# A two-layer decoder trunk: the turned copy of h in front of the gated input embedding is made through memory instead of on TensorE

## The chip, the cores and the metric

The kernel runs on one core of a Trainium2 chip. The metric is the device time of one execution in microseconds (us): the median of three runs before the change is 986.39 us (985.43 to 986.48). The profile shows one further execution, taken by the hardware profiler. Engines are named as the profile names them: PE is TensorE (PEld its weight loads), DVE is VectorE, ACT is ScalarE, POOL is GpSimd, and SP is the queue that issues nearly all transfers.

## The reference

The reference computes two layers over 256 tokens of width 1024 in float32. A layer has a gated feed-forward block (FFN 1), a token mixer, a second feed-forward block (FFN 2) and a gated per-layer input embedding. The change lies where the last two meet:

```python
h = h + 0.5 * swiglu(rms_norm(h, ffn2_norm), ffn2_w_gate, ffn2_w_up, ffn2_w_down)

gate = jax.nn.sigmoid(rms_norm(h, ple_norm) @ w_ple_gate)
h = h + gate * (p_i @ w_ple_proj)
```

`w_ple_gate` is 1024 x 1024 and `w_ple_proj` 256 x 1024. After the second layer a last RMS norm gives the output.

## The kernel before, in words

**Numbers.** Each float32 operand of a matmul is split into a high part and a remainder (tile names end in h and l), and each product is three matmuls: high times high, high times low, low times high (`mm3`, lines 263 to 268). So each piece of weights needs two instructions after it has landed: ACT copies the high part (`wh`, line 161) and DVE subtracts it to get the low part (`wl`, line 162). A piece is 128 x 1024 numbers, 512 KB, loaded by one transfer on SP (line 157) into one of seven raw buffers; the parts go into one of eight pairs of part buffers. The raw buffer comes free when `wl` is done, the part buffers when the last matmul has read them.

**Tiles.** The 256 tokens are two tiles t = 0 and 1 of 128. h is kept with tokens on partitions, in two halves f of 512 columns each. As the stationary operand of a matmul it must stand the other way round, with its columns on partitions: x, in parts h and l, eight chunks k of 128 columns. `turn_h` (line 379) makes one tile and half of x: four PE transposes (line 385) into one PSUM bank, four ACT copies that scale by the norm's gain (line 390, tile `xf`), an ACT copy to the high part (line 392) and a DVE subtraction for the low part (line 393).

**The end of FFN 2.** Its last product runs in `lagging` (line 423): four chunks of weights for tile 0, and the same four for tile 1, three chunks later. Each chunk and tile is six matmuls into two PSUM banks. When a tile's last chunk is done, `residual` (line 412) adds the two banks to h on DVE (line 416), and puts `turn_h` for both halves on a list of things to be emitted a little later, counted in matmul time (`soon`, `tick`); the turns of tile 0 fall between tile 1's last matmuls, those of tile 1 among the first matmuls of the next stage. ACT also sums the squares of h for the norm (`junk`, line 354), whose factor is applied later, as the scale of the sigmoid.

**The gates.** `ple` (line 1083) loops over halves f of the output columns and, within, over tiles t. Each half first computes the projection of the extra input p, `pv`, twelve matmuls for both tiles, and then for each tile the gate `e`: 8 chunks k x 3 = 24 matmuls over all of x. So the first half's gate weights (two units of two pieces) serve both tiles before the second half's are needed. Behind each `e` come the sigmoid on ACT (`se`, line 1113), the product with `pv` on DVE (`me`, line 1115) and the sum into h (line 1116). In the first layer each new part of h is then turned on PE for the next layer (`xt_e`); in the second, the last one, it is scaled and leaves.

**What sets the order.** The program is written as one sequence; a scheduler puts each engine's instructions into a fixed order, shown below where it changes, and every engine follows its own in order. The gates inside the FFNs already go through memory in the way that the change now uses for h (lines 549 to 558): DVE turns 32 x 32 blocks (`STREAM_TRANSPOSE`), one transfer writes the tile to memory (`m`), and four transfers of 64 KB read it back rearranged (`ft`).

## Time and profile before

| what | value |
|---|---|
| median of three runs | 986.39 us |
| profiled execution, its own time | 986.46 us |
| its span | 984.7 us |
| PE busy | 974.3 us (99%) |
| DVE busy | 844.6 us (86%) |
| ACT busy | 640.9 us (65%) |
| transfers | 208.32 MB, mean 212 GB/s |
| granted TensorE clock | 0.998 of full speed |

The busy time of PE says little, since matmuls overlap: one of 512 columns lasts 0.39 us in the records, but the next starts 0.227 us after it. A lost time on PE shows as a larger distance between two starts, and the prediction reads these distances. The first layer's stretch from the end of FFN 2 to the end of the gates lies at 451 to 493 us, the second layer's at 936 to 977 us. In names of tiles in the profile the layer is left out of some: d_b and xt_b belong to FFN 2, pv and e to the gates, g_a to the next FFN 1.

### The profile page before, as it was taken

How to read it: one execution, taken by the hardware profiler on the slowest of the kernel's cores; microseconds unless marked ns; L12 is line 12 of the kernel's file. 1: busy time of each engine (PE TensorE's matmuls, PEld its weight loads, DVE VectorE, ACT ScalarE, POOL GpSimd, SP SyncE). 2: the span in 40 equal slices, each digit the busy share in tenths (PEclk: the TensorE clock that was granted, in tenths of full speed). 3: DMA queues.
4: the chain of work that ended last, by engine and by line, in shares of the span. 5: the costliest groups of instructions: out<-in, count | busy, mean ns of one | idle time of the engine just before them, and what ended most of it. 6: DMA issues, size and time to landing. Idle time of an engine off the chain costs nothing.

```text
span 984.7 us, 13887 instructions
## 1 busy us (share of the span) xinstructions
PE 974.3 (99%) x4872; PEld 821.3 (83%) x4872; DVE 844.6 (86%) x1035; ACT 640.9 (65%) x958; POOL 39.1 (4%) x55
## 2 busy tenths in 40 slices
PE   9999999999999999999999999999999999999996
PEld 8888888899888888887878888889998888888885
DVE  5799899966789998989889989998666999987994
ACT  6756566857596556557866655667757865755673
POOL 0000000100110000000110000001010100000010
PEclk9999999999999999999999999999999999999999
DMA  8948766763065878576748786668602667876551
GB/s 300 357 159 295 243 198 216 262 227 109 23 234 157 268 254 276 156 246 215 256 144 278 227 277 212 210 213 299 210 27 86 214 205 243 278 239 207 200 199 43
DMA packets 85173, 208.32 MB, mean 212 GB/s; under 512 B 13680, under 2 KB 33264, under 8 KB 85104
## 3 DMA queue, kind: packets, MB, share of 16 engines
q1 hardware_dynamic: 84672, 206.87, 63.2%
q8 instruction: 38, 0.62, 0.3%
q10 hardware_dynamic: 432, 0.57, 0.2%
q14 instruction: 31, 0.25, 0.1%
HBM read 195.87 MB, written 11.53 MB: 211 GB/s over the span
## 4 chain that ended last, share of the span: by engine, by line
PE 80%; DVE 9%; DMA 4%; ACT 3%; issue 3%; SPq 0%; POOL 0%; POOLq 0%; DVEq 0%; ACTq 0%
DMA raw<-in_w 3%; PE g_a L267 3%; PE g_a L265 3%; PE g_a L266 3%; PE p_a L267 3%; PE p_a L266 3%; PE p_a L265 3%; PE d_a L267 3%; PE d_a L265 3%; PE d_a L266 3%; PE u_a L266 3%; PE u_a L265 3%; PE u_a L267 3%; PE p_b L265 3%; PE p_b L267 2%
## 5 line engine op out<-in xcount | busy, mean ns | idle before, releaser
L162 DVE TENSOR_TENSOR wl<-raw,wh 128x1024 fp32r<-128x1024 f32 (+1 forms) x278 | 320.7, 1186 | 56.1 <-ACT wh L161 55.0
L161 ACT ACTIVATE wh<-raw 128x1024 fp32r<-128x1024 f32 (+1 forms) x278 | 279.0, 1035 | 83.1 <-DMA raw<-in_w 19.4
L202 ACT ACTIVATE wh<-raw 128x1024 fp32r<-128x1024 f32 x133 | 139.4, 1060 | 128.8 <-DVE raw L197 75.5
L203 DVE TENSOR_TENSOR wl<-raw,wh 128x1024 fp32r<-128x1024 f32 x133 | 159.8, 1217 | 13.4 <-ACT wh L202 12.0
L197 DVE TENSOR_TENSOR raw<-raw,raw 128x1024 f32<-128x1024 f32 x76 | 92.6, 1220 | 4.8 <-DMA raw<-in_w 4.1
L265 PE MATMUL d_a<-wh,fh_a 128*128 128x512 f32 x108 | 42.4, 392 | 0.0
L266 PE MATMUL d_b<-wl,fh_b 128*128 128x512 f32 x108 | 42.2, 391 | 0.1
L267 PE MATMUL d_b<-wh,fl_b 128*128 128x512 f32 x108 | 42.3, 391 | 0.0
L265 PE MATMUL d_b<-wh,fh_b 128*128 128x512 f32 x108 | 42.2, 391 | 0.0
L267 PE MATMUL d_a<-wh,fl_a 128*128 128x512 f32 x108 | 42.1, 389 | 0.0
L266 PE MATMUL d_a<-wl,fh_a 128*128 128x512 f32 x108 | 42.0, 389 | 0.0
L265 PE MATMUL g_a<-wh,x0h 128*128 128x512 f32 x80 | 31.2, 393 | 0.0
L267 PE MATMUL g_a<-wh,x0l 128*128 128x512 f32 x80 | 31.0, 390 | 0.0
L266 PE MATMUL g_a<-wl,x0h 128*128 128x512 f32 x80 | 31.0, 389 | 0.0
L266 PE MATMUL u_a<-wl,x0h 128*128 128x512 f32 x64 | 25.0, 391 | 0.0
L265 PE MATMUL u_a<-wh,x0h 128*128 128x512 f32 x64 | 25.0, 394 | 0.0
L265 PE MATMUL g_b<-wh,x_mix1h 128*128 128x512 f32 x64 | 25.0, 391 | 0.0
L265 PE MATMUL g_b<-wh,x_mix0h 128*128 128x512 f32 x64 | 25.0, 391 | 0.0
L266 PE MATMUL g_b<-wl,x_mix1h 128*128 128x512 f32 x64 | 25.0, 391 | 0.0
L265 PE MATMUL g_a<-wh,xe0h 128*128 128x512 f32 x64 | 25.0, 391 | 0.0
L266 PE MATMUL g_b<-wl,x_mix0h 128*128 128x512 f32 x64 | 25.0, 390 | 0.0
L267 PE MATMUL u_a<-wh,x0l 128*128 128x512 f32 x64 | 24.9, 390 | 0.0
(527 smaller groups left out, 2672.1 us busy)
## 6 DMA issues: line engine op xcount, KB each, us to landing
raw<-in_w SPq DMA_DIRECT2D x338, 512.0 KB, 5.4
m_b<-pr_b SPq DMA_DIRECT2D x20, 256.0 KB, 2.3
ft_b<-m_b SPq DMA_DIRECT2D x80, 64.0 KB, 3.2
raw<-in_w SPq DMA_DIRECT2D x16, 256.0 KB, 5.0
m_a<-pr_a SPq DMA_DIRECT2D x16, 256.0 KB, 2.5
ft_a<-m_a SPq DMA_DIRECT2D x64, 64.0 KB, 2.8
xin<-in_xT SPq DMA_DIRECT2D x4, 256.0 KB, 5.0
h<-in_xr SPq DMA_DIRECT2D x2, 512.0 KB, 8.9
```

The source lines that it names most:

```text
L161: nc.scalar.activation(wh[:, a], r[:, a], AF.Copy),
L162: nc.vector.tensor_tensor(wl[:, a], r[:, a], wh[:, a].bitcast(F32), ALU.subtract),
L197: nc.vector.tensor_tensor(self.raw[o], self.raw[a], self.raw[b], op)
L202: newest_wh[0] = nc.scalar.activation(wh, r, AF.Copy)
L203: nc.vector.tensor_tensor(wl, r, wh.bitcast(F32), ALU.subtract)
L265: nc.tensor.matmul(o, ah, bh, start=start, stop=False, **kw)
L266: nc.tensor.matmul(o, ah, bl, start=False, stop=False, **kw)
L267: newest_mm[0] = nc.tensor.matmul(o, al, bh, start=False, stop=stop, **kw)
```

## The change

`move_h` takes the place of `turn_h` behind FFN 2. For each tile and half DVE turns the blocks into a buffer `hb`, a transfer writes it to memory (`mh`, 256 KB), and, after a delay, four transfers read it back (`hf`, 64 KB each); ACT scales `hf` in place, four instructions, and copies the high part, and DVE subtracts. The columns of x stand in another order than before, so the rows of the gate weights and the gains are permuted to match, ahead of the launch. The lag in front of it goes from 3 chunks to 4, so all of tile 0's chunks stand before tile 1's. In `ple` the projection `pv` is computed for both halves and both tiles at once, 24 matmuls; then the loop runs over tiles outside and halves inside, so all four units of gate weights are needed within tile 0. The transfers of the second half's weights stand behind the reads of tile 0 (`load_fence`). The delays of the turns for the next layer change.

```diff
+        def fetch(self, q, i):
...
+            newest_load[0] = nc.sync.dma_start(r, w[self.u, :, a : a + n])
+            if load_fence[0] is not None:
+                after(newest_load[0], load_fence[0])
...
+    def move_h(x, t, n, gcol, name):
...
+        pr = flat("w1", f"hb{t}{n}_{name}")
+        turned = nc.vector.transpose(pr, h[:, t, half(n)])
+        m = mem_p.tile([P, 4, P], F32, tag="turn", name=f"mh{t}{n}_{name}")
+        nc.sync.dma_start(m, pr.rearrange("p (q r) -> p q r", q=4))
+        a = wt("w2", f"hf{t}{n}_{name}", 4, P)
+
+        def back():
+            for q in range(4):
+                i = nc.sync.dma_start(a[32 * q : 32 * q + 32], m[:, q].rearrange("(a f) r -> f a r", a=4))
+            if t == 0:
+                newest_back[0] = i
+
+        def parts():
+
+            f = a.rearrange("p a (j s) -> p j a s", j=4)
+            c = gcol + 4 * n
+            for j in range(4):
+                nc.scalar.activation(f[:, j], f[:, j], AF.Copy, scale=g_sb[:, c + j : c + j + 1])
+            xh, xl = (in_runs(q) for q in both(x, slice(None), slice(4 * n, 4 * n + 4), slice(t * P, (t + 1) * P)))
+            two = nc.scalar.activation(xh, f, AF.Copy), nc.vector.tensor_tensor(xl, f, xh.bitcast(F32), ALU.subtract)
...
+        soon(BACK + 0.1 * n, back)
+        soon(PARTS + 0.1 * n, parts)
...
-            soon(wait[f], lambda f=f: turn_h(x, t, f, gcol, tag))
+            if far:
+                done = move_h(x, t, f, gcol, tag)
+            else:
+                soon(wait[f], lambda f=f: turn_h(x, t, f, gcol, tag))
...
-        return lagging(rest, d, gates, 0.5, tag, gcol, 3, False)
+
+        return lagging(rest, d, gates, 0.5, tag, gcol, 3 if between is None else 4, False, between is not None)
...
-        for f in range(2):
-            c = half(f)
-            wf = wide([Unit(4) for _ in range(2)])
-            v = [bank(f"pv{L}{f}{t}") for t in range(2)]
-            for k in range(2):
-                for t in range(2):
-                    mm3(v[t], tok(xp, k, t), up.at(k, c.start, c.stop), k == 0, k == 1, skip_group_check=True)
+        us = [[Unit(4) for _ in range(2)] for f in range(2)]
+        wf = [wide(u) for u in us]
+        up.ready()
+        us[0][0].ready()
+        for q in range(2):
+            us[0][1].fetch(q, 0)
+
+        load_fence[0] = newest_back[0]
+        for u in us[1]:
+            for q in range(2):
+                u.fetch(q, 0)
+        v = [[bank(f"pv{L}{f}{t}") for t in range(2)] for f in range(2)]
+        for k in range(2):
             for t in range(2):
+                for f in range(2):
+                    mm3(v[f][t], tok(xp, k, t), up.at(k, f * 512, (f + 1) * 512), k == 0, k == 1, skip_group_check=True)
+        for t in range(2):
+            for f in range(2):
+                c = half(f)
...
-                        soon(4.4 if f == 0 else 2.8, lambda t=t, f=f: turn_h(nx, t, f, gcol, f"e{L}"))
+                        soon(4.4 if t else 7.0 - f, lambda t=t, f=f: turn_h(nx, t, f, gcol, f"e{L}"))
```

The change moves instructions on three engines. The places below are those of the first layer, where FFN 2 meets the gates; the second layer's read alike. In the names, d_b000 to d_b011 are the PSUM banks of tile and half, 80 is the unit of the projection's weights, 81 and 82 are those of the first half's gates, 83 and 84 of the second half's, and the digit behind the unit is the piece. First DVE. Before:

```order
L416 SCALAR_TENSOR_TENSOR h_84<-d_b000_3969,h_84 128x512
L416 SCALAR_TENSOR_TENSOR h_84<-d_b001_3970,h_84 128x512
L162 TENSOR_TENSOR wl80_0_0_198_4485<-raw80_0_0_198_4486,wh80_0_0_198_4484 128x1024
L162 TENSOR_TENSOR wl80_1_0_199_4509<-raw80_1_0_199_4510,wh80_1_0_199_4508 128x1024
L416 SCALAR_TENSOR_TENSOR h_84<-d_b010_3971,h_84 128x512
L393 TENSOR_TENSOR x_b0l_4387<-xf00_b0_4433,x_b0h_4386 128x4x128
L416 SCALAR_TENSOR_TENSOR h_84<-d_b011_3972,h_84 128x512
L162 TENSOR_TENSOR wl81_0_0_200_4534<-raw81_0_0_200_4535,wh81_0_0_200_4533 128x1024
```

On the same engine at the same place, now:

```order
L457 SCALAR_TENSOR_TENSOR h_84<-d_b000_3969,h_84 128x512
L457 SCALAR_TENSOR_TENSOR h_84<-d_b001_3970,h_84 128x512
L409 STREAM_TRANSPOSE hb00_b0_4415<-h_84 128x512
L409 STREAM_TRANSPOSE hb01_b0_4421<-h_84 128x512
L457 SCALAR_TENSOR_TENSOR h_84<-d_b010_3971,h_84 128x512
L457 SCALAR_TENSOR_TENSOR h_84<-d_b011_3972,h_84 128x512
L172 TENSOR_TENSOR wl80_0_0_333_4489<-raw80_0_0_334_4486,wh80_0_0_333_4488 128x1024
L409 STREAM_TRANSPOSE hb10_b0_4465<-h_84 128x512
L409 STREAM_TRANSPOSE hb11_b0_4471<-h_84 128x512
L172 TENSOR_TENSOR wl80_1_0_335_4495<-raw80_1_0_336_4492,wh80_1_0_335_4494 128x1024
L172 TENSOR_TENSOR wl81_0_0_337_4501<-raw81_0_0_338_4498,wh81_0_0_337_4500 128x1024
L172 TENSOR_TENSOR wl81_1_0_339_4507<-raw81_1_0_340_4504,wh81_1_0_339_4506 128x1024
```

The two low parts of unit 80 have moved from ahead of tile 1's sums to behind them, and four block transposes have come in. Next PE, from the last matmul of FFN 2 on. Before:

```order
L266 MATMUL d_b011_3972<-wl79_1_0_197_4368,fh_b0_4_3854 128x512
L267 MATMUL d_b011_3972<-wh79_1_0_197_4367,fl_b0_4_3855 128x512
L265 MATMUL pv000_4482<-wh80_0_0_198_4484,xpsbk0_4263 128x512
L266 MATMUL pv000_4482<-wl80_0_0_198_4485,xpsbk0_4263 128x512
L267 MATMUL pv000_4482<-wh80_0_0_198_4484,xpv0_4264 128x512
L265 MATMUL pv001_4483<-wh80_0_0_198_4484,xpsbk0_4263 128x512
```

On PE, now:

```order
L276 MATMUL d_b011_3972<-wl79_1_0_331_4370,fh_b0_4_3854 128x512
L277 MATMUL d_b011_3972<-wh79_1_0_331_4369,fl_b0_4_3855 128x512
L275 MATMUL pv000_4522<-wh80_0_0_333_4488,xpsbk0_4263 128x512
L275 MATMUL pv010_4524<-wh80_0_0_333_4488,xpsbk0_4263 128x512
L275 MATMUL pv001_4523<-wh80_0_0_333_4488,xpsbk0_4263 128x512
L275 MATMUL pv011_4525<-wh80_0_0_333_4488,xpsbk0_4263 128x512
L276 MATMUL pv000_4522<-wl80_0_0_333_4489,xpsbk0_4263 128x512
```

Four matmuls that need only the high part now stand before the first that reads `wl80`. Last the SP queue, which before held only weight loads here (unit 82, then 83 and on). Now:

```order
L155 DMA raw82_1_0_342_4512<-in_w 128x1024
L411 DMA mh00_b0_4417<-hb00_b0_4415 128x512
L411 DMA mh01_b0_4423<-hb01_b0_4421 128x512
L416 DMA hf00_b0_4419<-mh00_b0_4417 32x4x128 x4
L416 DMA hf01_b0_4425<-mh01_b0_4423 32x4x128 x4
L411 DMA mh10_b0_4467<-hb10_b0_4465 128x512
L411 DMA mh11_b0_4473<-hb11_b0_4471 128x512
L155 DMA raw83_0_0_343_4514<-in_w 128x1024
L155 DMA raw83_1_0_344_4516<-in_w 128x1024
L155 DMA raw84_0_0_345_4518<-in_w 128x1024
L155 DMA raw84_1_0_346_4520<-in_w 128x1024
L416 DMA hf10_b0_4469<-mh10_b0_4467 32x4x128 x4
```

The four loads of the second half's weights have moved behind the writes of all of h and the reads of tile 0, and ahead of the reads of tile 1.

More of the change, by code (lines that the diff above doesn't have):

```diff
@@ L135, in trunk @@
     newest_load, newest_wh, newest_wl = [None], [None], [None]
+    load_fence, newest_back, far_parts = [None], [None], [None, None]
     fence = [None, None]
@@ L146, in __init__ @@
             self.sub, self.cut = sub, cut
-            self.parts, self.here = {}, set()
+            self.parts, self.here, self.raw = {}, set(), {}
+        def fetch(self, q, i):
+            n = PIECE // self.sub
+            name = f"raw{self.u}_{q}_{i}_{next(ids)}"
+            r = self.raw[q, i] = raw_p.tile([P, PIECE], F32, tag="raw", name=name)[:, :n]
+            a = q * PIECE + i * n
+            newest_load[0] = nc.sync.dma_start(r, w[self.u, :, a : a + n])
+            if load_fence[0] is not None:
+                after(newest_load[0], load_fence[0])
         def load(self, q, i):
             name = f"{self.u}_{q}_{i}_{next(ids)}"
+            if (q, i) not in self.raw:
+                self.fetch(q, i)
             if q not in self.parts:
@@ L154, in load @@
             wh, wl = (t[:, i * n : (i + 1) * n] for t in self.parts[q])
-            r = raw_p.tile([P, PIECE], F32, tag="raw", name=f"raw{name}")[:, :n]
-            a = q * PIECE + i * n
-            newest_load[0] = nc.sync.dma_start(r, w[self.u, :, a : a + n])
+            r = self.raw.pop((q, i))
             for c in range(self.cut):
@@ L393, in turn_h @@
         nc.vector.tensor_tensor(xl, f, xh.bitcast(F32), ALU.subtract)
+    def move_h(x, t, n, gcol, name):
[16 more added lines that the diff above has]
+            two = nc.scalar.activation(xh, f, AF.Copy), nc.vector.tensor_tensor(xl, f, xh.bitcast(F32), ALU.subtract)
+            if t == n == 0:
+                fence[:] = two
+            far_parts[:] = two
+        soon(BACK + 0.1 * n, back)
+        soon(PARTS + 0.1 * n, parts)
+        return turned
     def column(r, name, behind):
@@ L410, in four, with residual @@
         return [[bank(f"{name}{t}{n}") for n in range(2)] for t in range(2)]
-    def residual(x, n, d, t, scale, tag, gcol, wait=(1.2, 1.9)):
+    def residual(x, n, d, t, scale, tag, gcol, far, wait=(1.2, 1.9)):
         for f in range(2):
@@ L421, in residual, with lagging @@
         return done
-    def lagging(chunks, d, x, scale, tag, gcol, lag, first=True, behind=True):
+    def lagging(chunks, d, x, scale, tag, gcol, lag, first=True, far=False, behind=True):
         nx, nn = new_x(f"x_{tag}"), Norm(tag)
@@ L432, in lagging @@
                     if c == N - 1:
-                        done = residual(nx, nn, d, t, scale, tag, gcol)
+                        done = residual(nx, nn, d, t, scale, tag, gcol, far)
                         if t == 0 and behind:
@@ L1063, in mix @@
         rest = [(us[2 + i // 2], i % 2, 4 + i) for i in range(4)]
-        return lagging(rest, d, Of(y), 1.0, f"mix{L}", g0 + G_FFN2, 4, False, False)
+        return lagging(rest, d, Of(y), 1.0, f"mix{L}", g0 + G_FFN2, 4, False, behind=False)
     def ple_inputs(L):
@@ L1108, in ple @@
                     for k in range(KC):
-                        mm3(e, tok(x, k, t), both(wf(k), slice(None), p), k == 0, k == KC - 1, skip_group_check=True)
-                    if f == t == 0:
-                        flush()
+                        mm3(e, tok(x, k, t), both(wf[f](k), slice(None), p), k == 0, k == KC - 1, skip_group_check=True)
                     s = flat("w0", f"se{L}{f}{t}{a}")[:, :step]
@@ L1114, in ple @@
                     m = flat("w1", f"me{L}{f}{t}{a}")[:, :step]
-                    nc.vector.tensor_tensor(m, v[t][:, p], s, ALU.mult)
+                    product = nc.vector.tensor_tensor(m, v[f][t][:, p], s, ALU.mult)
+                    if f and not t:
+                        after(sig, far_parts[0])
+                        after(product, far_parts[1])
                     nc.vector.tensor_tensor(hc, m, hc, ALU.add)
@@ L1120, in ple @@
                     else:
-                        soon(4.4 if f == 0 else 2.8, lambda t=t, f=f: turn_h(nx, t, f, gcol, f"e{L}"))
-                if f:
-                    nn.done(t)
-                    if last:
-                        leave(hg, nn, t)
+                        soon(4.4 if t else 7.0 - f, lambda t=t, f=f: turn_h(nx, t, f, gcol, f"e{L}"))
+            nn.done(t)
+            if last:
+                leave(hg, nn, t)
         if not last:
@@ L1233, in _weights, with _far @@
         for m in range(0, DM, 512):
-            wide(i["w_ple_gate"][L], ar(m, m + 512))
+            wide(i["w_ple_gate"][L][_far()], ar(m, m + 512))
     return np.stack(units)
+def _far():
+    import numpy as np
+    return np.concatenate([k + turned_order(512) for k in range(0, DM, 512)])
 def _gains(i):
@@ L1241, in _gains @@
     names = ("ffn1_norm", "mix_norm", "q_lat_norm", "kv_lat_norm", "sb_out_norm", "mla_out_norm", "ffn2_norm", "ple_norm")
-    g = [i[n][L].reshape(-1, P) for L in range(DEPTH) for n in names] + [i["final_norm"].reshape(-1, P)]
+    g = [i[n][L][_far() if n == "ple_norm" else slice(None)].reshape(-1, P) for L in range(DEPTH) for n in names] + [i["final_norm"].reshape(-1, P)]
     return np.ascontiguousarray(np.concatenate(g).T)
```

## The prediction

> **What bounds the kernel now.** I read the page's busy times first, then the busy time in a stretch over the place of the change, then PE's own timeline there, start by start.
>
> ```profile
> PE 974.3 (99%) x4872; PEld 821.3 (83%) x4872; DVE 844.6 (86%) x1035; ACT 640.9 (65%) x958; POOL 39.1 (4%) x55
> ...
> 460.00:480.00 20.00, 19.89 (x96) 15.75 (x95) 18.28 (x20) 17.60 (x43) 3.81 (x4) 1.00 0.71 238
> ```
>
> In the row of the stretch the columns are the stretch, its length, then busy time (and count) of PE, PEld, DVE, ACT and POOL, the granted clock, the transfers' share and GB/s. PE is busy for 19.89 of 20 us, but DVE is for 18.28 as well. So PE sets the end, and taking work from it pays, provided DVE, which gets more work, doesn't become what PE waits for. PE's timeline (start, duration, line, tile) shows what the removed transposes cost:
>
> ```profile
> 460.25 0.39 PE L266 MATMUL d_b<-wl,fh_b 128*128 128x512 f32 x1
> 460.48 0.60 PE L385 MATMUL xt_b<-c_sb,h 128*128 128x128 f32 x4
> 460.83 0.48 PE L267 MATMUL d_b<-wh,fl_b 128*128 128x512 f32 x1
> 461.15 0.60 PE L385 MATMUL xt_b<-c_sb,h 128*128 128x128 f32 x4
> 461.50 0.48 PE L265 MATMUL d_b<-wh,fh_b 128*128 128x512 f32 x1
> 461.82 0.39 PE L266 MATMUL d_b<-wl,fh_b 128*128 128x512 f32 x1
> ...
> 462.75 0.39 PE L267 MATMUL d_b<-wh,fl_b 128*128 128x512 f32 x1
> 462.98 0.39 PE L265 MATMUL pv<-wh,xpsbk 128*128 128x512 f32 x1
> ```
>
> Undisturbed starts are 0.227 us apart (460.25 to 460.48, 462.75 to 462.98). From 460.25 to 461.82 are three such steps, 0.68 us, and it took 1.57: the two groups of four transposes cost 0.89.
>
> **What the change takes away.** Two more groups stand among the `pv` matmuls, one wait in the first gate block, and one in the next FFN:
>
> ```profile
> 464.11 0.40 PE L267 MATMUL pv<-wh,xpv 128*128 128x512 f32 x1
> 464.35 0.60 PE L385 MATMUL xt_b<-c_sb,h 128*128 128x128 f32 x4
> 464.70 0.48 PE L265 MATMUL pv<-wh,xpsbk 128*128 128x512 f32 x1
> 465.02 0.39 PE L266 MATMUL pv<-wl,xpsbk 128*128 128x512 f32 x1
> 465.25 0.40 PE L267 MATMUL pv<-wh,xpv 128*128 128x512 f32 x1
> ...
> 466.31 0.39 PE L266 MATMUL pv<-wl,xpsbk 128*128 128x512 f32 x1
> ...
> 469.71 0.63 PE L265 MATMUL e<-wh,x_b0h 128*128 128x512 f32 x2
> 470.45 0.50 PE L266 MATMUL e<-wl,x_b0h 128*128 128x512 f32 x1
> 470.78 0.40 PE L267 MATMUL e<-wh,x_b0l 128*128 128x512 f32 x1
> ...
> 472.83 0.39 PE L267 MATMUL e<-wh,x_b0l 128*128 128x512 f32 x1
> ...
> 493.33 0.39 PE L265 MATMUL g_a<-wh,xe0h 128*128 128x512 f32 x1
> ...
> 496.51 0.39 PE L267 MATMUL g_a<-wh,xe0l 128*128 128x512 f32 x1
> 497.37 0.66 PE L385 MATMUL xt_e<-c_sb,h 128*128 128x128 f32 x4 [0.48 <-DVE h L1116]
> 497.79 0.48 PE L265 MATMUL g_a<-wh,xe0h 128*128 128x512 f32 x1
> 498.10 0.39 PE L266 MATMUL g_a<-wl,xe0h 128*128 128x512 f32 x1
> ```
>
> 464.11 to 465.02 is 0.91 for two steps, so 0.45 more than they need; 465.25 to 466.31 is 1.06, 0.60 more; 469.71 to 470.78 is 1.07 for three steps, 0.39 more, a wait for a low part of weights. The last four rows: 1.59 for two steps, 1.14 more, of which 0.45 is the group itself, which stays; the other 0.69 is a wait for h. The turn is now emitted 4.4 us of matmul time behind the last gate instead of 2.8, and h came 4.0 us behind it (497.37 against 493.33), so that wait goes. First layer: 0.89 + 1.05 + 0.39 + 0.69 = 3.0. The second layer has no next FFN; I take its groups as the first's, 2.3. **Gain: 5.4 us**, if nothing takes the place of the two waits. PE's other matmuls stay as many.
>
> **What it adds.** I follow the first layer on the clock of these rows. With two groups fewer, the first `pv` starts at T0 = 462.98 - 0.89 = 462.09.
>
> ```profile
> 459.26 1.28 DVE L416 SCALAR_TENSOR_TENSOR h<-d_b,h 128x512 f32<-128x512 f32 x2
> 460.46 2.35 DVE L162 TENSOR_TENSOR wl<-raw,wh 128x1024 fp32r<-128x1024 f32 x2
> ...
> 469.18 2.35 DVE L162 TENSOR_TENSOR wl<-raw,wh 128x1024 fp32r<-128x1024 f32 x2
> 471.45 0.68 DVE L393 TENSOR_TENSOR x_b0l<-xf_b,x_b0h 128x512 fp32r<-128x512 f32 x1
> ```
>
> Before, the low parts of the projection's weights were made at 460.46, ahead of tile 1's sums. Now they stand behind these, and those wait for FFN 2's last matmul. In a row of DVE a small instruction takes 0.60 and a `wl` 1.14 (459.26 + 2 x 0.60 = 460.46; two `wl` 2.27), 0.68 and 1.21 until its own end. Tile 1's last sum can start some 0.28 behind T0: a gate's last matmul started at 472.83 and its sigmoid, on ACT, at 473.32, 0.49 later, of which 0.227 is the step to the next matmul. So `wl` of the projection's first piece ends at T0 + 0.28 + 0.60 + 1.21 = T0 + 2.1, and PE goes on some 0.06 later (469.18 + 1.21 = 470.39, and PE at 470.45). Only four matmuls, 0.91, stand ahead: **PE waits 1.24.** The second piece stands behind two block transposes: T0 + 2.03 + 1.2 + 1.21 = 4.45; PE needs it after 11 more matmuls, at 4.65, so no wait. The gates could start at 2.15 + 20 x 0.227 = T0 + 6.7.
>
> Is x there? The same way through memory, of the FFN's gates:
>
> ```profile
> 311.22 1.29 DVE L549 STREAM_TRANSPOSE pr_b<-pr_b 128x512 f32<-128x512 f32 x2
> 311.94 0.92 SPq L551 DMA_DIRECT2D m_b<-pr_b  x2
> 314.46 3.64 SPq L556 DMA_DIRECT2D ft_b<-m_b  x8
> ...
> 319.83 0.64 ACT L532 ACTIVATE fh_b<-ft_b 128x512 fp32r<-128x512 f32 x1 [0.50 <-DMA ft_b<-m_b]
> ft_b<-m_b SPq DMA_DIRECT2D x80, 64.0 KB, 3.2
> raw<-in_w SPq DMA_DIRECT2D x338, 512.0 KB, 5.4
> ```
>
> The transposes, the two writes, the eight reads, and the copy that waited for the last read. It started 8.6 us after the first transpose, and 2.15 after the last read was issued (issues 0.46 apart, the eighth at 317.67). The first half's fourth read, issued at 315.83, would so have landed at 318.0, 6.8 after the first transpose. Tile 0's transposes now start behind its two sums, at 460.46 = T0 - 1.63, so the halves land at about T0 + 5.2 and T0 + 7.0. In the second layer one load of 512 KB more stands between; I take it as nothing and keep it for the range. On ACT:
>
> ```profile
> 473.32 0.69 ACT L1113 ACTIVATE se<-e,hr_b 128x512 f32<-128x512 f32 x1 [1.60 <-PE e L267]
> ...
> 480.37 2.02 ACT L161 ACTIVATE wh<-raw 128x1024 fp32r<-128x1024 f32 x2
> ...
> 498.07 1.14 ACT L390 ACTIVATE xf_e<-xt_e,g_sb 128x128 f32<-128x128 f32 x4
> 499.24 0.64 ACT L392 ACTIVATE xe0h<-xf_e 128x512 fp32r<-128x512 f32 x1
> ```
>
> Four scales and the high copy take 1.17 + 0.64 = 1.8, so the first half's high part is there at T0 + 7.0, or 6.5 if it lands half a us sooner than the quoted one: PE waits 0 to 0.36, I take 0.2. Its low part follows on DVE 0.7 later, and the third matmul needs it 0.45 after the start: 0.27. ACT then makes two `wh` (2.02) and only then the second half: its high part at T0 + 10.2 to 10.7, where PE, 12 matmuls on, is at T0 + 9.7 to 10.0: 0.6, and 0.28 for the low part. The first gate block ends, the sigmoid and the product run, and behind them stand the last two pieces of weights: `wh` after the sigmoid (0.26 + 0.65 + 1.06), `wl` 1.21, ready 3.2 after the block's end, needed 2.96 after: 0.28; the last piece, behind the sum into h, 0.37 more. Tile 1's x waits on ACT behind the square of the new h, which waits for that sum: about 0.53 at its first block. **Loss in a layer: 1.24 + 0.2 + 0.27 + 0.6 + 0.28 + 0.65 + 0.53 = 3.8, in both 7.5 us.**
>
> Of the rest: ACT's scales are as many as before. The four block transposes (1.29 for two) give DVE 2.4 us more a layer, in a stretch in which it idles 1.7 of 20 (first rows), so up to 0.7 can be left over for the next FFN; PE waits there only if DVE's lead is used up, and I take nothing, with 0.7 in the range. The 20 added issues of each layer on SP are hidden by the loads' lead, but for the second half's four loads, which now go out from about T0 + 5.5: by the page's 5.4 they land from T0 + 10.9 on, and ACT comes to them at 10.5, so 0.4 or, if they land one behind the other at a later pace, 1 to 2 us may be lost; I take nothing. The tail behind the last gate hangs on that gate alone, as before.
>
> [...]
>
> **Sum.** 986.46 (the profiled execution, 0.07 above the median) - 5.4 + 7.5 = 988.6; taken to the median, 988.5 us.
>
> **Rivals.** A measurement of this kernel tells about 0.2%, 2.0 us, from no change, so the lines are 984.4 and 988.4 us.
>
> *Even.* The transfers land sooner: in SP's order no load of weights stands among them, whereas the quoted chain is one execution's of many and may have had some beside it. Then the first block loses 0.5 instead of 1.35 and tile 1 0.25: 2.6 a layer, 986.46 + 5.3 - 5.4 = 986.3. Against it: ACT's order, two `wh` ahead of the second half, holds whatever the transfers do.
>
> *Faster.* PE profits fully where DVE isn't late: only the wait for the projection's low part, 1.24, and a quarter us elsewhere: 986.46 + 3.0 - 5.4 = 984.1. It decides if `wl` and x stand ready at the gates' first matmul; against it are the 18.28 of 20 us.
>
> *Much slower.* The reads of tile 0 land as late as under load (3.2 and more instead of 2.1, and the write as well), or the four late loads take the page's 5.4: 2 us more a layer, 992.5.
>
> *It doesn't take the way said.* The loads of the second half could still run ahead of the reads; but SP's order puts them behind, and it issues in order. I give it nothing.
>
> **How the numbers follow.** Forecast 0.55, even 0.25, faster 0.12, much slower 0.08. The forecast's own range, with 3.2 to 4.6 lost in a layer, is 987.3 to 990.1, and a bit over a third of it (0.2) lies below 988.4. So slower 0.35 + 0.08 = 0.43, same 0.2 + 0.25 = 0.45, faster 0.12. The range that leaves out 2 in 10 is 985.0 to 991.0.
>
> **What would show it.** PE: no xt_b; a distance of some 1.4 us between the fourth and fifth `pv` start, ended by DVE `wl`; about 1.3 us of waits in the first gate block, half of it ended by ACT's x in the middle; 0.65 in the second block ended by `wl`; no wait at the next FFN's turn. From T0 to the next FFN's first matmul about 32.7 us (30.35 - 1.05 - 0.39 + 3.8) instead of 30.35. The prediction is wrong if the `pv` wait is missing, or if the blocks of gates run at 0.227 us a matmul: then the even or the faster case holds.

## The result, and the profile after

The changed kernel took 992.84 us (median of 4 runs, 990.73 to 994.3) beside 986.43 for the kernel before (985.43 to 987.5): a ratio of 1.0064, 95% interval 1.0052 to 1.0077. It is slower by 6.4 us, where 2 were forecast, and the time lies above the range of 985.0 to 991.0 that was given. A second series gave 992.19 (5 runs, 990.88 to 993.2) and 1.0059 [1.0046, 1.0072]. The profiled execution is one of 992.08 us (span 990.3, granted clock 0.998).

The page's busy times, and the list of what PE waited for (total us, times, longest):

```profile
PE 975.2 (98%) x4840; PEld 817.2 (83%) x4840; DVE 849.2 (86%) x1043; ACT 641.4 (65%) x958; POOL 35.3 (4%) x55
...
PE pv L276 <- DVE wl L172: 2.0, 2, 1.0
PE e L276 <- DVE wl L172: 1.3, 2, 0.8
...
PE v L275 <- ACT x_a1h L402: 0.5, 1, 0.5
...
PE e L275 <- ACT x_b0h L427: 0.4, 1, 0.4
PE e L275 <- ACT x_b1h L427: 0.4, 1, 0.4
```

The 32 transposes are gone from PE (4872 instructions before, 4840 now), and its busy time is no shorter. The waits list holds what was forecast (low parts of weights among `pv`, x in the middle of the first gate block) and one place that was not: `v`, the first matmul of the next layer's mixer, 200 us behind the changed place.

PE's timeline in the first layer (start, duration, line, tile):

```profile
462.58 1.07 PE L275 MATMUL pv<-wh,xpsbk 128*128 128x512 f32 x4
464.68 0.50 PE L276 MATMUL pv<-wl,xpsbk 128*128 128x512 f32 x1 [1.03 <-DVE wl L172]
...
473.17 0.50 PE L275 MATMUL e<-wh,x_b0h 128*128 128x512 f32 x1 [0.45 <-ACT x_b0h L427]
...
480.09 0.50 PE L276 MATMUL e<-wl,x_b0h 128*128 128x512 f32 x1 [0.58 <-DVE wl L172]
...
482.62 0.50 PE L276 MATMUL e<-wl,x_b0h 128*128 128x512 f32 x1 [0.76 <-DVE wl L172]
...
496.52 0.40 PE L275 MATMUL g_a<-wh,xe0h 128*128 128x512 f32 x1
```

The `pv` wait, the wait in the middle of the first block and the two in the second stand where the forecast put them. From the first `pv` to the next FFN it is 33.94 us; forecast 32.7, before 30.35.

I matched PE's matmuls in the timelines of both kernels by the tile they write and their number, and took how far each is shifted. The steps of this shift, in us, for both profiled executions of the changed kernel:

| stretch | forecast | first profile | second profile |
|---|---|---|---|
| start to 451 us, nothing changed there | 0 | +0.5 | -0.2 |
| FFN 2's last chunks, first layer | -0.9 | -0.9 | -0.9 |
| `pv` and gates, first layer | +2.3 | +3.6 | +3.0 |
| next FFN's last turn | -0.7 | -0.7 | -0.7 |
| second layer's first FFN, mixer, second FFN | 0 | +0.9 | +1.0 |
| FFN 2's last chunks, second layer | -0.9 | -0.9 | -0.9 |
| `pv`, gates and tail, second layer | +2.3 | +3.1 | +3.1 |
| sum | +2.2 | +5.6 | +4.4 |

The gains came as forecast, to a tenth of a us. What is missing lies in the gates and, without any term of mine, in the 440 us between them; the first profile has 0.5 more ahead of the changed place. Both profiles lie below their series' medians, so a further us or so of a typical execution is not accounted for by these columns.

What each part of the gates loses, counted as its length less 0.227 us a matmul (24 `pv`, then blocks of 12):

| part | forecast | first layer | second layer |
|---|---|---|---|
| `pv` and the wait for x ahead of the gates | 1.44 | 1.42 | 1.59 |
| first half of the first block and the wait at its middle | 0.87 | 1.01 | 1.01 |
| its second half | 0.28 | 0.40 | 0.40 |
| second block | 0.65 | 2.16 | 0.96 |

The last term, 0.53 at tile 1's first block, is smaller than forecast: in the first layer that block loses 0.77, of which 0.45 is a group of four transposes for the next layer, which the kernel before has as well, and 0.3 is waiting. So one term is far off, the second block. Its loads, on SP's queue (two writes of h, eight reads, two writes, the four loads, tile 1's eight reads, the next FFN's eight loads), behind it ACT's high parts made from those four loads:

```profile
461.76 0.92 SPq L411 DMA_DIRECT2D mh_b<-hb_b  x2
463.80 3.64 SPq L416 DMA_DIRECT2D hf_b<-mh_b  x8
467.54 0.38 SPq L411 DMA_DIRECT2D mh_b<-hb_b  x1
468.01 0.38 SPq L411 DMA_DIRECT2D mh_b<-hb_b  x1
468.48 2.15 SPq L155 DMA_DIRECT2D raw<-in_w  x4
470.74 9.47 SPq L416 DMA_DIRECT2D hf_b<-mh_b  x8
...
480.25 10.34 SPq L155 DMA_DIRECT2D raw<-in_w  x8
```

```profile
473.51 1.06 ACT L171 ACTIVATE wh<-raw 128x1024 fp32r<-128x1024 f32 x1 [0.40 <-DMA raw<-in_w]
475.48 1.06 ACT L171 ACTIVATE wh<-raw 128x1024 fp32r<-128x1024 f32 x1 [0.90 <-DMA raw<-in_w]
...
477.71 1.06 ACT L171 ACTIVATE wh<-raw 128x1024 fp32r<-128x1024 f32 x1 [0.47 <-DMA raw<-in_w]
480.25 1.06 ACT L171 ACTIVATE wh<-raw 128x1024 fp32r<-128x1024 f32 x1 [1.47 <-DVE wl L172]
```

The first three landed at 473.4, 475.4 and 477.6: 5.0 us behind the issue for the first, and then one every 2.1 us (1.2 and 2.7 us apart in the second profile). PE is through with a piece in 6 matmuls, 1.36 us. That is the case that the prediction named ("one behind the other at a later pace, 1 to 2 us") and costed at nothing.

The same queue shows the second thing missed. Before, the next FFN's eight loads followed at once:

```profile
468.46 11.53 SPq L157 DMA_DIRECT2D raw<-in_w  x8
```

Now they go out 11.8 us later (480.25), on a PE that is some 3 us later. What SP waited for between 455 and 495 us, and what became of it at the end of the second layer's first FFN (DVE's first sum into h there, before and after; PE's next mixer, after):

```profile
SPq L416 <- DMA raw<-in_w: 5.1, 3, 1.9
```

```profile
649.01 0.69 DVE L723 SCALAR_TENSOR_TENSOR h<-p_a,h 128x512 f32<-128x512 f32 x1 [0.44 <-ACT u_a L726]
```

```profile
655.41 0.68 DVE L767 SCALAR_TENSOR_TENSOR h<-p_a,h 128x512 f32<-128x512 f32 x1
...
671.58 0.50 PE L275 MATMUL v<-wh,x_a1h 128*128 128x512 f32 x1 [0.53 <-ACT x_a1h L402]
```

Before, DVE had a lead there, that is, it was through with the work ahead of this sum before the sum's operand was there: it waited 0.44 us, up to 649.01. Now it comes 6.4 us later, without waiting, while PE there is 2.7 later: the lead is gone, h is summed late, its turns are late, and the next mixer waits for x.

### The profile page after: what moved, and what is told of

The parts are those of the page before. It is cut to its first block, busy times and chain, and to the rows that moved or that the text cites. A ratio compares the mean times of both kernels' runs of the same rounds, so it can differ in the third digit from the quotient of the medians.

```text
span 990.3 us, 13925 instructions
## 1 busy us (share of the span) xinstructions
PE 975.2 (98%) x4840; PEld 817.2 (83%) x4840; DVE 849.2 (86%) x1043; ACT 641.4 (65%) x958; POOL 35.3 (4%) x55
## 4 chain that ended last, share of the span: by engine, by line
PE 77%; DVE 10%; DMA 5%; ACT 4%; issue 3%; SPq 1%; POOL 0%; POOLq 0%; DVEq 0%; ACTq 0%
PE g_a L277 3%; PE g_a L276 3%; PE g_a L275 3%; PE p_a L275 3%; PE p_a L276 3%; PE p_a L277 3%; DMA raw<-in_w 3%; PE g_b L277 3%; PE g_b L275 3%; PE g_b L276 3%; PE u_a L276 3%; PE u_a L277 2%; PE u_a L275 2%; PE d_a L277 2%; PE d_a L275 2%
## 5 line engine op out<-in xcount | busy, mean ns | idle before, releaser
L277 PE MATMUL g_b<-wh,x_mix1l 128*128 128x512 f32 x64 | 25.2, 393 | 0.0
```

What stands on the lines that cost most here:

```text
L277: newest_mm[0] = nc.tensor.matmul(o, al, bh, start=False, stop=stop, **kw)
```

## The experiments

Each was timed in five rounds beside the kernel before; ratios are to it, and rows are of the run's own profile, PE's timeline where nothing else is said. "Changed" is the changed kernel. Some products of the FFNs are made by Strassen's scheme: seven products of sums of blocks in place of eight products of blocks. DVE makes these sums, those over raw weights among them, and the names "Strassen operand" and "Strassen product" below mean its parts.

**Again.** The changed kernel, unaltered.

> The changed kernel itself, unaltered, a second time, so that the others have a partner on the same chip, and to see which of its waits come back. Theory 'orders' (the loss is made by what stands behind what: the projection's low parts behind tile 1's sums, the second half's loads behind the reads, tile 1's reads in front of the next loads): 992 to 993.5 us, and in the first layer the second gate block loses 1.5 to 2 us again, ended by low parts of weights whose loads came late. Theory 'chance' (the profiled execution was an unlucky one, the four late loads don't normally cost more than the 0.65 I forecast): the second block loses 0.5 to 0.8 and the median is 990 to 991. The 0.6 us that were lost ahead of the changed place are expected to be gone under both.

Measured 992.19 us, 1.0059 [1.0046, 1.0072]. The second block lost 1.96 in the first layer and 0.96 in the second: not chance. Only the 0.5 ahead of the changed place did not come back. A loss in the next FFN did, at another place (PE's timeline of the second profile):

```profile
567.42 0.50 PE L275 MATMUL p_a<-wh,xe0h 128*128 128x512 f32 x1 [0.57 <-DVE ch_a L668]
```

**The fence removed.**

```
-        load_fence[0] = newest_back[0]
```

> The changed kernel without the fence that puts the second half's four loads behind tile 0's reads. Seven raw buffers let one of the four go out early, ahead of h's transfers; the other three stay where they were. Theory 'orders': the four pieces land about 2.1 us apart, so the last three land one place sooner, the second gate block loses 0.3 instead of 2.0 in the first layer and 0.2 instead of 0.8 in the second: 2 us less than the changed kernel, 990.8. Rival 'contention': 512 KB more on the way beside h's write and reads make tile 0's x late by up to 2 us, and what the second block gains the first one loses: 992 to 994.

Measured 993.37 us, 1.0070 [1.0058, 1.0083]: not faster. Yet the second block's loss is 0.01 in the first layer and 0.04 in the second, and the shift at the next FFN's first matmul is 0.6 instead of 1.9 to 3.2. The loss came back 200 us later: 2.6 us where the next mixer begins, on the list of PE's waits partly as

```profile
PE v L275 <- ACT x_a1h L402: 1.1, 1, 1.1
...
PE q L276 <- DVE x_a1l L403: 0.7, 1, 0.7
```

So the fence does cost what the second block lost. A part of it is paid back at once: the first block loses 0.4 to 0.6 us a layer more than in the changed kernel (PE waits 0.68 at 472.54 for ACT's `wh`). Contention, the rival's cause, is little of that: tile 0's reads landed 2.0 us behind their issue in the first layer, as with the fence, and 3.2 against 2.8 in the second. What becomes of the rest is decided elsewhere.

**The projection's low parts first.** `up` is made and its weights split ahead of tile 1's last chunk:

```
+                    ahead and t == 1 and c == N - 1 and ahead()     # ups.append(Unit(2).ready())
                     down_mm(d, u, j, x(k), x.at(k), t, first and c == 0, c == N - 1)
-        up = Unit(2)
+        up = ups.pop()
```

> The changed kernel with the low parts of the projection's weights made ahead of tile 1's two sums and two transposes on DVE, instead of one behind the sums and one behind the transposes. Nothing else moves. Theory 'orders': the wait of 1.3 us among the pv matmuls goes in both layers and nothing takes its place, since tile 1's x, now 2.3 us later at its start, is needed only some 20 us on: 2.6 us less than the changed kernel, 990.2. Rival 'it moves on': the gates then start 1.3 us sooner and wait as much longer for tile 0's x, which comes from memory at a time that the pv matmuls don't set: no more than 0.5 us less, 992.3 or more, and the wait at the first gate is about 1.8 us instead of 0.47.

Measured 991.17 us, 1.0051 [1.0038, 1.0065]. Among the `pv` there is no wait any more, and the first gate starts no sooner:

```profile
468.80 0.50 PE L275 MATMUL e<-wh,x_b0h 128*128 128x512 f32 x1 [0.86 <-ACT x_b0h L427]
```

From the first `pv` to the first gate 1.15 us are lost in the first layer (1.30 in the second profile of the changed kernel) and 1.58 in the second (1.55). The rival's mechanism is right: x through memory is not there sooner, and the wait moved to it. Its time (992.3 or more) did not come: the median is 1 us below the changed kernel's, though the intervals overlap.

**Tile 1's reads into other buffers.**

```
-        a = wt("w2", f"hf{t}{n}_{name}", 4, P)
+        a = wt("w3" if t else "w2", f"hf{t}{n}_{name}", 4, P)
```

> The changed kernel with the reads of tile 1 into another pair of buffers, so that they don't wait until tile 0's x has been made from the first pair. SP issues in order, and in the changed kernel the next FFN's first eight loads stood behind these waiting reads and went out from 480.3 us on, against 468.5 before the change. Theory 'orders': they go out some 5 us sooner, and the 0.3 us at tile 1's first block, and part of the 0.7 that the second layer loses between the gates and its own place, are won: 991.5 to 992.2. Rival 'cover': nobody waits for these loads, and the time is that of the changed kernel within 0.3 us.

Measured 990.74 us, 1.0044 [1.0032, 1.0057]. The reads hardly got sooner: in the changed kernel only 0.4 us of SP's waiting there was for these buffers, and 5.1 for the four loads to land. The next FFN's loads went out at 477.8, 1.2 to 2.4 us sooner and not 5, so my reason for this run was wrong. The median is 1.5 to 2.1 us below the two of the changed kernel, with intervals that overlap. Its profile, of the fastest execution (988.6), has the second block lose 1.0 instead of 2.0 and no wait at tile 1's first block; whether that is the buffers' doing is not shown.

**Tile order with PE turns.** `far` off, the rows of the gate weights in their own order, no fence, and without the two ordering edges that the change has between tile 1's x and the second gate of tile 0:

```
-... 3 if between is None else 4, False, between is not None)
+... 3 if between is None else 4, False, False)
```

> The order of the changed kernel (all 24 pv matmuls first, then the gates tile by tile, the second half's loads requested beside the first's, the later delays of the turns in front of the next FFN) with h turned by PE as before the change: no block transposes, nothing through memory, no fence on the loads. Theory 'orders and lead': the loss belongs to the way through memory (DVE's four transposes, loads behind reads), so here it is gone, the 0.7 us of the next FFN's turn are won, and the time is 985.3 to 987 us. Rival 'demand': the tile order itself asks DVE for all eight pieces of gate weights in 10.9 us instead of some 16, and a part of the loss stays: 988 us or more, with waits for low parts in the second gate block.

Measured 987.64 us, 1.0013 [1.0004, 1.0021]. The order itself is no loss: the gates' stretch gains 0.4 us in each layer against before. What it loses is one wait in the next FFN, behind a DVE that stood in its queue at a sum whose load had not landed (PE's row, then DVE's):

```profile
500.36 0.66 PE L395 MATMUL xt_e<-c_sb,h 128*128 128x128 f32 x4 [1.68 <-DVE h L1174]
```

```profile
496.14 1.23 DVE L207 TENSOR_TENSOR raw<-raw,raw 128x1024 f32<-128x1024 f32 x1 [1.88 <-DMA raw<-in_w]
```

So some 5 of the 6 us belong to the way through memory (its transposes, its transfers and the fence together).

**DVE's added work alone**, in the kernel before:

```
+            tag[0] == 'b' and nc.vector.transpose(flat('w1', ...), h[:, t, c])
             soon(wait[f], lambda f=f: turn_h(x, t, f, gcol, tag))
```

> The kernel before the change with one block transpose of each half of h added on DVE behind each of FFN 2's four last sums, its result unused: the work that the way through memory adds to DVE (2.4 us a layer), without the way. Theory 'lead': DVE runs through the next FFN with hardly a gap, so what it loses at the gates isn't made good, and PE pays a part of it, at the pv matmuls and gates and again where the next FFN ends: 1 to 3 us over both layers, 987.4 to 989.4. Rival 'cover', which the prediction took (nothing, 0.7 at most): 986.2 to 987.1.

Measured 993.1 us, 1.0075 [1.0056, 1.0095]: 2.4 us of DVE work a layer cost more than itself, at one place in each layer:

```profile
468.59 0.51 PE L266 MATMUL pv<-wl,xpsbk 128*128 128x512 f32 x1 [2.67 <-DVE wl L162]
```

In the next FFN DVE was in step (2.9 us later at its first sum into h, as was PE).

**Tile 0's h sent earlier**, with the projection's low parts first: tile 1's Strassen sums moved behind tile 0's transposes.

```
+        def second():
+            ...v, b and to_h(1, 0, v), to_h(1, 1, b), called behind tile 0's transposes
```

> The changed kernel with the low parts of the projection's weights ahead of tile 1's sums, as in the run before, and in FFN 2's end the sums of the Strassen products that belong to tile 1's rows behind tile 0's block transposes instead of ahead of them: tile 0's h leaves some 2 us sooner. With the low parts alone the first gate waited for x from memory as long as the pv matmuls had waited before. Theory 'orders': now both waits go, 1.5 to 2.5 us a layer less than in the changed kernel: 987.5 to 989.5. Rival 'loads': the second half's weights come no sooner, and the second block waits for what the first one saves: no more than 1 us less than the changed kernel, 991 us or more.

Measured 994.16 us, 1.0079 [1.0067, 1.0092]. The writes went out 2.7 us sooner (458.2 against 460.9 in the second profile), but ACT, in order, made two of the four scales, then stood at the square of tile 1's h (which now came later), and made the other two behind it (ACT's timeline):

```profile
464.32 0.69 ACT L425 ACTIVATE hf_b<-hf_b,g_sb 128x128 f32<-128x128 f32 x2 [4.81 <-DMA hf_b<-mh_b]
465.97 0.63 ACT L364 ACTIVATE junk_b<-h 128x512 bf16<-128x512 f32 x1 [0.96 <-DVE h L457]
...
467.22 0.68 ACT L425 ACTIVATE hf_b<-hf_b,g_sb 128x128 f32<-128x128 f32 x2
```

So it does not test what it was made for. Whether an earlier h would pay with ACT's order mended was not tried.

**Tile 1's reads from GpSimd's queue.**

```
-                i = nc.sync.dma_start(a[32 * q : 32 * q + 32], ...)
+                i = (nc.gpsimd if t else nc.sync).dma_start(a[32 * q : 32 * q + 32], ...)
```

> The changed kernel with tile 1's eight reads of h issued from GpSimd's queue instead of SP's. In the changed kernel SP stood from 470.7 to 479.5 us at these reads, waiting mostly for the four big loads in front of them to land (5.1 us in 3 waits), and the next FFN's loads stood behind. Theory 'lead': these now go out as soon as a buffer is free, some 5 us sooner, DVE idles 2 to 3 us less between 462 and 500, and what PE loses in the next FFN (0.2 to 0.9 at its second Strassen product and 0.6 at the next mixer's first matmul) goes: 1 to 1.5 us less than the changed kernel, 990.7 to 991.2. Rival 'buffers': the loads wait for free raw buffers anyway, 992 to 992.8.

Measured 1000.4 us, 1.0138 [1.0125, 1.0151]. The next FFN's loads did go out early, from 470.1 us (480.25 in the changed kernel), as 'lead' had it. But ACT's order had changed. It stood 3.5 us at tile 1's scales, with the high part of a gate piece that had landed at 476.6 behind them, and PE waited 3.8 for that:

```profile
480.13 1.29 ACT L425 ACTIVATE hf_b<-hf_b,g_sb 128x128 f32<-128x128 f32 x4 [3.48 <-DMA hf_b<-mh_b]
481.34 1.04 ACT L171 ACTIVATE wh<-raw 128x1024 fp32r<-128x1024 f32 x1
```

After this wait PE's starts were 0.43 us apart up to 488.2, at a granted clock of 0.65 from 480 to 485 and 0.67 from 485 to 490, which costs another 2.2 us. The queue itself isn't the cause. Count, KB and median us to landing of the reads of h, first tile 0's on SP and tile 1's on GpSimd's queue (POOLq) in this run, then tile 1's on SP in the changed kernel:

```profile
hf_b<-mh_b SPq DMA_DIRECT2D x8, 64.0 KB, 2.0
hf_b<-mh_b POOLq DMA_DIRECT2D x8, 64.0 KB, 7.5
...
hf_b<-mh_b SPq DMA_DIRECT2D x8, 64.0 KB, 7.5
```

Behind the four loads the reads take 7.5 us on either queue: they landed from 477.6 to 483.0 us here and from 480.1 to 482.1 in the changed kernel. So the run doesn't test what earlier loads for the next FFN are worth.

**SP's order in the next FFN tied to the old one**, in the changed kernel and in the one without the fence: 114 transfers from the first Strassen load of the second layer's first FFN on, each put behind the one ahead of it in the order of before.

```
+        its = [spq[c].pop(0) for c in want]
+        [after(q, p) for p, q in zip(its, its[1:])]
```

> The changed kernel with SP's order in the second layer's first FFN (loads, and the gates' own writes and reads, 114 transfers) tied to the order that the kernel before had there. Nothing else is tied. Without it the scheduler, whose own clock the change had moved, put loads of the Strassen operands there behind reads of the gates, some 130 us behind the changed place, and DVE came 2.2 to 3.7 us later to the end of that FFN than PE; where the order was the old one (the tile order with PE turns, and the kernel before with added transposes) DVE was in step. Theory 'far order': DVE is in step again (its first sum into h no more than 1 us later than PE's own delay), the 0.6 us at the next mixer's first matmul and most of the 0.2 to 0.9 at 565 us go: 0.8 to 1.5 less than the changed kernel, 990.7 to 991.4. Rival 'late start': DVE's lateness comes from the loads that left the gates' stretch late, and stays whatever the order: 992 to 992.8.

> The same tie, in the kernel without the fence on the second half's loads. There the second gate block of the first layer had already gained 1.4 us, and 2.6 us were lost at the end of the second layer's first FFN instead, where the scheduler had chosen yet another order. Theory 'far order': that loss goes, the gain stays, and the time is about 1.4 us below the run with the tie alone: 989.3 to 990.3. Rival 'late start': 992.5 or more.

Measured 992.88 us, 1.0057 [1.0044, 1.0070], and 990.34 us, 1.0035 [1.0021, 1.0048]. Under the fence the tie brings nothing, and DVE's first sum into h came at 656.40, as late as without it: there the order is not the cause. Without the fence it brings 3 us. With the order held equal, the fence costs 2.5 us; these two runs are the fair comparison of the fence, and the first pair was not. DVE is late in both (652.62 without the fence, on a PE 0.4 us ahead of before), so the fence alone doesn't take its lead.

**Tile order with PE turns, and the sums held back** behind the gates' last sum into h:

```
-            nc.vector.tensor_tensor(self.raw[o], self.raw[a], self.raw[b], op)
+            i = nc.vector.tensor_tensor(...); last_h[0] is not None and after(i, last_h[0])
```

> The tile order with PE turns, and the sums over raw Strassen operands held behind the gates' last sum into h on DVE. In the run without this DVE stood 1.9 us at such a sum, whose load hadn't landed, in front of the last gate's product, and PE waited 1.68 us for h at the next FFN's last turn. Expected: that wait goes, the gates' own gain of 0.4 us in each layer stays: 985.4 to 986.3 us. Rival: the Strassen operands come as much later, and the wait moves to their product: 987 to 988.

Measured 986.1 us, 0.9995 [0.9986, 1.0003], 11 runs. The wait of 1.68 is gone. It is the best version found, and not measurably better than before.

**The later turn alone**, in the kernel before:

```
-                    soon(4.4 if f == 0 else 2.8, ...)
+                    soon(4.4, ...)
```

> The kernel before the change with one number altered: the turn of the last half of each tile in front of the next FFN 4.4 us of matmul time behind its gate instead of 2.8. It tests the prediction's term of 0.69 by itself. Expected: PE's wait for h at that turn goes and nothing else: 985.5 to 986.1 us. Rival: x of the last half comes later by as much and PE waits there instead: 986.3 to 986.8.

Measured 986.72 us, 1.0001 [0.9993, 1.0010]. The turn's wait is gone and PE is 0.6 us ahead of before until the next FFN's Strassen product, where it waits for DVE and is level with before again (565.91 there):

```profile
565.90 0.50 PE L265 MATMUL p_a<-wh,xe0h 128*128 128x512 f32 x1 [0.23 <-DVE ch_a L624]
```

**DVE's work alone, the projection first**: the run with unused transposes and the edit of "low parts first" together.

> The kernel before with the four unused block transposes a layer on DVE, as in the run before, but with the low parts of both pieces of the projection's weights ahead of tile 1's sums and transposes. In that run PE waited 2.65 us in each layer for the second piece, 5.3 of the 6.6 us, and DVE was in step with PE through the whole next FFN. Theory 'place': the same work costs next to nothing where it doesn't stand ahead of what PE needs next: 986.5 to 988 us. Rival 'amount': DVE has no room for 2.4 us more a layer, and the wait comes back at the gates: 990 us or more.

Measured 993.64 us, 1.0068 [1.0054, 1.0083]. The `pv` run through; now tile 1's sums, their turns and x stand behind, and PE waits at the gates (its timeline, and the row of a stretch as in the prediction):

```profile
469.50 0.50 PE L265 MATMUL e<-wh,x_b0h 128*128 128x512 f32 x1 [2.11 <-ACT x_b0h L392]
...
471.14 0.63 PE L267 MATMUL e<-wh,x_b0l 128*128 128x512 f32 x1
471.56 0.63 PE L265 MATMUL e<-wh,x_b0h 128*128 128x512 f32 x1
...
470.00:475.00 5.00, 5.00 (x16) 3.95 (x16) 5.00 (x6) 1.68 (x3) 0.00 (x0) 0.66 0.72 214
```

So the amount counts, not only the place: in both orders DVE had no room between FFN 2's end and the first gate. Part of this run's loss is something else: matmul starts are 0.43 us apart from 470.3 to 473.7, at a granted clock of 0.66 over the five us of the row, which costs 1.6 us there.

**The transfers alone**: the best version, with h also written and read back, straight from h into buffers that nobody reads (they take turns with those of ACT's squares and DVE's sums), with the fence and without it. No DVE work is added, and x comes from PE.

```
-        pr = flat("w1", ...); turned = nc.vector.transpose(pr, h[:, t, half(n)])
+        pr = h[:, t, half(n)]
         ...the write and the four reads stay; the x made from them goes
```

> The tile order with PE turns and the held-back sums (986.1 us), and beside it h written to memory and read back as in the changed kernel, straight from h and into buffers that nobody uses, with the second half's four loads behind tile 0's reads. So it has the changed kernel's transfers and late loads, but no transposes on DVE, and x comes from PE as before. Theory 'lost lead': the second gate block loses 1 to 2 us in the first layer and 0.5 to 0.8 in the second, DVE comes to the next FFN 3 to 5 us later against PE than without, and PE pays another 0.5 to 1.5 there: 988 to 990. Rival 'x alone' (the loss hangs on x's and the projection's lateness): 986 to 987.

> The same without the fence: one of the four loads goes out ahead of tile 0's reads. Theory 'lost lead': one place sooner in the row of loads is worth 1 to 2 us of it: 986.8 to 988.3, and less than with the fence by at least 0.7. Rival 'x alone': as with the fence, within 0.5 us.

Measured 993.14 us, 1.0067 [1.0055, 1.0079], and 990.73 us, 1.0040 [1.0028, 1.0052]: 7 us and 4.6 more than the same kernel without them. In the first layer's gates PE falls 0.2 us behind the kernel before and in the second's 1.8. The second block, fenced here too, loses 0.2 us in the first layer where the changed kernel lost 2: its four loads go out at 467.0, 1.5 us sooner, and land by 478.0. In the next FFN PE falls 5 us behind, between 561 and 574 us, in waits for weights:

```profile
564.05 0.50 PE L275 MATMUL p_a<-wh,xsh_a 128*128 128x512 f32 x1 [0.86 <-ACT wh L212]
...
573.57 0.50 PE L276 MATMUL p_a<-wl,xe0h 128*128 128x512 f32 x1 [0.82 <-DVE wl L172]
```

The size exceeds what I expected; the place is the next FFN, 70 us behind the transfers. But the scheduler had laid out that FFN anew. On SP two of the four pieces of a Strassen operand stand behind a gate's reads, where the kernel without these transfers has all four ahead of the reads, the last one issued at 540.2; and on DVE the last two of the operand's four sums stand behind another gate's product and turn (SP's rows, then DVE's, of the run with the fence):

```profile
541.27 0.40 SPq L204 DMA_DIRECT2D raw<-in_w  x1
543.00 3.64 SPq L600 DMA_DIRECT2D ft_a<-m_a  x8
546.73 0.85 SPq L204 DMA_DIRECT2D raw<-in_w  x2
```

```profile
559.30 1.29 DVE L593 STREAM_TRANSPOSE pr_a<-pr_a 128x512 f32<-128x512 f32 x2
560.52 1.19 DVE L213 TENSOR_TENSOR wl<-raw,wh 128x1024 fp32r<-128x1024 f32 x1
561.63 2.48 DVE L207 TENSOR_TENSOR raw<-raw,raw 128x1024 f32<-128x1024 f32 x2
```

The last piece had landed at 552.5, 9 us ahead of these two sums; without the transfers the four sums were done at 550.9. PE's wait at 564.05 is for the part made from the first of the two. So this wait at least hangs on an order and not on a late load. How much of the 5 us is lead that the transfers took is not shown, since SP's order was not tied in these kernels.

## Why the prediction was wrong

The direction and most of the mechanisms at the place were right, and the size was too small: 2 us were forecast and 6.4 measured. Two steps failed, the term for the second gate block and the sentence that lets the loads' lead hide the added transfers.

- *The gains* (0.89, 1.05, 0.39, 0.69) came. But the 0.69 is none: the later turn alone gives it back 70 us on, because PE there is within 0.6 us of DVE. I costed a wait that goes as a gain and did not ask who is next.
- *"PE waits 1.24"* among the `pv`, the first x 0.2 and 0.27, the second half 0.6 and 0.28: measured 1.42, 1.01 and 0.40 against 1.44, 0.87 and 0.28. That these terms may not be taken singly, the run with the low parts first shows: with 1.24 removed, x from memory takes its place.
- *The second block, 0.65,* was the mis-sized term: 2.16 and 0.96. It was built on ACT's and DVE's order alone. The sentence "0.4 or, if they land one behind the other at a later pace, 1 to 2 us may be lost; I take nothing" had the right answer in it and chose the wrong end. The rows of before showed the issue time (T0 + 5.5), eight reads ahead of the loads, and 512 KB apiece; what I did not work out was the pace, four loads at one each 2.1 us against PE's 1.36 us a piece. The profile's 5.4 us from issue to landing held for the first (5.0) and not for the fourth (9.9). Without the fence the block lost nothing; with SP's order held, the fence is worth 2.5 us.
- *"The 20 added issues of each layer on SP are hidden by the loads' lead"* is the step that failed altogether. I followed the loads that the gates need, and not the next FFN's eight, which stood behind tile 1's reads and went out 11.8 us later. At the end of that FFN DVE had lost 3.7 us against PE, and it was as late with SP's order tied to the old one, so the order is not what took the lead here. PE paid 0.9 to 1.0 us for it in the profiles. That the late loads took it, and not DVE's added work, is argued from the run with unused transposes, where DVE was in step; no run shows it by itself.
- *"Up to 0.7 can be left over for the next FFN; I take nothing"*: DVE's added work does not surface there (in the run with unused transposes it was in step), but at the gates at once, 2.1 to 2.7 us a layer.
- *The rival "much slower"* gave 992.5 and the cause, late loads, at a chance of 0.08. It is the case nearest to what came, but its number is met partly by luck: it has 2 us more in each layer's gates, and they lost 0.7 to 1.3 more, with the rest behind them. Tile 0's reads, which it has late too, landed 2.0 us behind their issue in the first layer and 2.8 in the second. The forecast's own text had the pieces for it in two places, each put at nothing, and the chances treated them as mishaps instead of as one cause: everything that leaves SP later.
- *Sums.* With 3.2 to 4.6 us lost in a layer, the forecast's terms give 987.4 to 990.2, not 987.3 to 990.1; nothing hangs on that.

What stays open: the losses of these runs don't add up. Unused transposes cost 6.6 us, unused transfers 7, both together with the gain of the turns 6. They may be paid from the same slack, and the scheduler lays out the next FFN anew for most of these kernels; which share of the changed kernel's loss is which is not settled. Some 1 us between the profiled executions and the medians is not accounted for either.

## What to carry to other kernels

SP issued in order, and its delay passed on to what stood behind: the next FFN's eight loads, behind tile 1's reads, went out 11.8 us later. When transfers are put ahead of loads, follow the loads not only to their next reader but to the end of the prefetch lead they keep up, and price the pace at which they land (here one each 2.1 us in the first profile) against the pace at which they are used (1.36 us a piece). A wait that is removed is worth only the distance to the next engine's own time (the later turn's 0.6 us was gone 70 us on, at a wait for DVE); where DVE and PE run within a us of each other, look for it before counting the gain. Compare two variants of a scheduled kernel only with the order of the far stages held equal, since an edit can reorder work 100 us away; the runs with the transfers alone did not hold it.

## What the runs showed of the hardware

- In the run with transposes and the projection first, PE waited 2.11 us; behind this wait starts were 0.43 us apart for 3.4 us (470.3 to 473.7), at a granted clock of 0.66 from 470 to 475. In its second layer, where the wait was 2.4 us, the clock was 0.84 from 955 to 960 and 0.82 from 960 to 965. In the run with reads on GpSimd's queue, a wait of 3.84 us was followed by such starts up to 488.2, at 0.65 from 480 to 485 and 0.67 from 485 to 490. The gap of 2.67 us in the other run with transposes was followed by 1.00 (470 to 475). So the clock was lower behind a wait of 2.11 us and not behind one of 2.67; what decides between them is not shown.
- The 64 KB reads of tile 1, issued behind four loads of 512 KB, landed 7.5 us (median) behind their issue from SP in the changed kernel, and 7.5 from GpSimd's queue in the run that moved them; tile 0's, issued from SP ahead of these loads, landed 2.0 behind. The medians show no difference between the two queues.
- Four loads of 512 KB issued within 2.2 us, next to writes and reads of h, landed 5.0 us behind for the first and then 2.0 to 2.3 us apart in the first profile, 1.2 to 2.7 in the second. Of the next seven, issued from 480.25 us, the last six landed 1.2 to 1.3 us apart in the first profile.
